# A decoder trunk on one core: who transposes the inverses and the delta rule's output, where the key scales are applied, and the order of the kernel's begin and of the ends of sums

## The chip, the core and the metric

One of the eight cores of a Trainium2 chip runs the whole kernel. The metric is device time in microseconds of one execution, taken as the median over several; a profile shows one execution in detail. The core's engines are TensorE (PE: matrix products and transposes into PSUM, its accumulator memory), VectorE (DVE), ScalarE (ACT), GpSimd (POOL) and SyncE (SP), which here issues nearly all DMAs. Each engine works off its own list of instructions in order and waits for the others by semaphores.

## The reference, cut to what matters

Two layers, 256 tokens of 1024 channels. Each layer is a half-step SwiGLU FFN, a mixer (gated DeltaNet beside a causal convolution module) and another FFN. What the change touches lies in the mixer's delta rule, for chunks of tokens with their decays `G`:

```
kk    = einsum("bhncd,bhnsd->bhncs", k, k)
a_mat = where(strict, kk * decay * beta[..., :, None], 0)
lhs   = eye + a_mat
rhs   = concatenate([v * beta[..., None], k * (beta * exp(G))[..., None]])
u, w  = split(triangular_solve(lhs, rhs, lower=True, unit_diagonal=True))
qk    = einsum("bhncd,bhnsd->bhncs", q, k) * decay
for each chunk:
    v_new = u_c - w_c @ state
    o_c   = q_c @ state + qk_c @ v_new
    state = state * d_c + k_c.T @ v_new
o = rmsnorm(o, norm_w) * silu(z);   y_a = o @ w_o
```

`q` and `k` are L2-normalised per head; there are 8 heads of 128. Each sub-layer ends as `x + r * rmsnorm(f(...), w_post)`, `r` 1/2 for the FFNs and 1 for the mixer.

## The kernel before

**Products.** All large products are float32 made of three passes: weights arrive by DMA as `raw`, ScalarE rounds them to `whi`, VectorE or GpSimd subtracts for `wlo` (`Stream`, lines 246 to 321), activations are split likewise, and `mm3` (543) issues hi x hi, hi x lo and lo x hi. `proj_in` (549) runs over column chunks of an input weight, `proj_out` (610) over contraction steps `kt` of an output weight, 16 x 3 products of 512 columns on the first block of 128 tokens and then as many on the second where there are only 8 steps.

**Order of the work.** TensorE takes its instructions in program order. The program's side work is written as generators ("jobs"), and `Lanes` (177) steps them between products: `lanes.tick()` is called after each group of three 512-column products, `DELAY` gives each job the ticks before its first step and between its steps, `AFTER` and `LATE` say which jobs must be done before and for how many ticks, `BEFORE` and `lanes.finish` force a job to its end at a fixed place, and `FILL` jobs (the 31-tap convolutions on VectorE, the inverse on GpSimd) are stepped whenever a rough model says that the engine has less than `ahead` microseconds of work in front of TensorE. `PLAN` (38) is the order of the mixer's 17 column chunks, with the jobs that each chunk's end starts. From the mixer's second chunk on, up to three chunks before its end, VectorE's and GpSimd's instructions keep program order (`in_order`, 103), and ScalarE's stay behind TensorE's (`Held`, 160); elsewhere a scheduler orders all engines but TensorE by priority and readiness.

**The delta rule.** Tokens are worked on in two blocks of 128 (`tb`), heads in two groups of four (`gp`). `k_tokens` (896) and `q_tokens` (1043) turn `k` and `q` by TensorE, square them and sum for the norms. `similarity` (920) makes `at`, multiplies by `sc` (the key's beta and inverse squared norm) and writes its 32x32 diagonal blocks to DRAM; `inverse` (950) inverts all of them at once on GpSimd and sends them back to `U` by way of DRAM, in eight DMAs per layer (line 974). `merge` (978) joins the blocks to 128x128 inverses by small products: its first four steps transpose `U` by TensorE, one step per head group and block, four heads each, and ScalarE copies three 32x32 diagonal blocks per head out of PSUM into `at`. `scan_first` and `scan_second` (1082, 1100) run the chunk recurrence; `head` (1074) makes four products into one PSUM bank and lets ScalarE copy it out as `vn`, `state` or `o`. The key scale `sc` is in `qk` (multiplied in on VectorE, one head at a time) and, times a decay, in `ktok` (through `kds`).

**The output.** `o_first` and `o_norm` (1288, 1292) norm and gate `o`, block by block; `o_norm` then transposes `o` by TensorE in four groups of four and splits the result to `oT` (`ot` in the profile). This job runs between the products of the convolution's output projection; the projection with `gdn_w_o` follows at once and reads `oT`.

**Begin and ends.** `start` (479) loads `x` in halves, transposes eight 128-column pieces of the first block, multiplies by the norm's weight into `xt`, and takes the first weight piece in two halves of the work but one DMA. `post` (529) ends each sub-layer: per half, a squared sum on ScalarE (`jk`, `ss`) and the weighted copy `fw` on VectorE; then `rms_scale` (414), a small sum on VectorE and a power on GpSimd (`rpost`), and the addition to `x`.

**The activations' turn, as it is.** In `ffn` (649) the gated activations are already transposed without TensorE: VectorE turns 32x32 blocks (`way`), four DMAs write them to DRAM, one reads them back in place.

Of the kernel before, what the change touches and what calls it, by code (L numbers as in the profile page):

```python
# [13 lines left out]
ALU = mybir.AluOpType  # L14
# [8 lines left out]
RING = 8  # L23
RMS_EPS = 1e-6
# [21 lines left out]
    "first": (1, 2), "ffn": (3, 5, 12), "pre0": (13, 7, 8, 4, 3, 3), "pre1": (15, 16, 0, 13, 8),  # L46
    "yt0": (10, 0, 10, 10, 26), "yt1": (10, 2, 0, 3, 3), "f_g0": (5, 0, 2, 1), "f_g1": (5, 1, 1, 1), "c0": (0, 0),
    "f_k1": (0, 1, 3, 1, 1, 3), "f_ka": (2, 0, 3), "decays": (12, 4, 2, 15, 4), "dts": (51, 3, 0, 0, 19, 19),
# [15 lines left out]
    "qs": ("qt0", "qt1"), "s0": ("merge", "vt0", "vt1", "qt0", "qt1"), "s1": ("s0",),  # L64
# [5 lines left out]
FILL = (("c3", "c2", "c1", "c0"), ("inv",))  # L70

LATE = {"inv": 20, "cn": 12, "sim0": 6, "sim1": 6, "merge": 7, "dts": 14}

POOL = {5, 7, 8, 11, 13, 16, *range(18, 21), 23, *range(29, 33), 35, 36, *range(39, 45), *range(47, 50), 51, 53, 55, 58, 60, 61, 63, 65, 67, 68, *range(70, 73), 77, 78, 84, 85}

CFG = dict(stat=500, conv=50, ev=300, tok=4, st=4, post=-800, pre=1000, fin=None, turn=None, tokens=-100, glu=100, dec=200, dts=-100, kt=-400, vt=1000, qt=50, inv=1000, sim=100, merge=-400, scan=50, norm=200, onorm=-100, yt=-400, w=50, tails=4, ahead=1.5, lag=6, free=3, aheadp=3, lag2=3, bias=2, held=1)

KIND = {"f_g0": "glu", "f_g1": "glu", "f_g2": "glu", "f_g3": "glu", "decays": "dec", "dts": "dts", "kt0": "kt", "kt1": "kt",
        "vt0": "vt", "vt1": "vt", "qt0": "qt", "qt1": "qt", "qs": "qt", "inv": "inv", "sim0": "sim", "sim1": "sim",
# [97 lines left out]
class Lanes:  # L177
# [13 lines left out]
    def step(self, job):  # L191
        try:
            with prio(self.tc, KIND.get(job[1])):
                next(job[3])
            job[2] += 1
# [50 lines left out]
class Stream:  # L246
# [16 lines left out]
    def load_one(self, parts=1):  # L263
# [5 lines left out]
        nc.sync.dma_start(raw[:, :n], src)  # L269
# [11 lines left out]
        if self.lanes is not None:  # L281
            c = slice(0, n)
            self.his.append((self.lanes.now + CFG["lag"], i, lambda: high(c)))
            self.lows.append((self.lanes.now + CFG["lag"] + CFG["lag2"], i, lambda eng: low(c, eng)))
            return
        for k in range(parts):
            if k:
                yield
            c = slice(k * n // parts, (k + 1) * n // parts)
            high(c)  # L290
# [1171 lines left out]
```

## Time and profile before

| | |
|---|---|
| median of 3 runs | 1355.97 us (1354.11 to 1357.88) |
| the profiled execution | 1356.38 us |
| its span, first to last instruction | 1354.4 us |
| mean granted TensorE clock | 0.998 |
| DMA: mean rate, HBM read | 202 GB/s, 256.68 MB |

A line of a group reads: source line, engine, operation, tiles written <- tiles read, shapes, count, then busy time in us, mean ns of one, and after the second bar the engine's idle time just before them with what ended it. Source lines 123, 143, 149 and 170 are the helpers through which all instructions of VectorE and GpSimd, all products, all transposes, and all of ScalarE pass, so groups are told apart by their tiles. A row of a timeline is: start, duration, engine, the same description, and in brackets the idle time before it. Products overlap in TensorE's pipeline, so the cost of one is read from start to start and not from its duration.

### The profile page before, as it was taken

To read this page: it belongs to the slowest core of one execution; us is meant where nothing else is said; L and a number is where in the kernel's file an instruction comes from. 1 tells how busy PE (TensorE), PEld (TensorE's weight loads), DVE (VectorE), ACT (ScalarE), POOL (GpSimd) and SP (SyncE) were. 2 spreads that over 40 slices of the span, in tenths; PEclk is the share of its full clock that TensorE was granted. 3 is DMA by queue.
4 is the path that set the end of the run, shared out by engine and by line. 5 is a ranking of instruction groups with operands and counts; after the bars stand their busy time and mean duration, and the time that the engine had idled before them with its cause. 6 is when DMAs were issued, how large, how long until landed. Compare 5 with 4: busy or idle time off the path is not lost.

```text
span 1354.4 us, 20203 instructions
## 1 busy us (share of the span) xinstructions
PE 1331.3 (98%) x7259; PEld 1132.3 (84%) x7259; DVE 926.9 (68%) x1593; ACT 730.8 (54%) x1172; POOL 446.4 (33%) x372
## 2 busy tenths in 40 slices
PE   9999999998999999999999999999989999999998
PEld 7888878997888888888888888799978878888886
DVE  6666456999966676765476654579999566766553
ACT  6554447666555545554455553577555564555541
POOL 0111025798834201111001110278986432011110
PEclk9999999999999999999999999999999999999999
DMA  7877745553634666876478775464545446477760
GB/s 273 284 259 248 232 164 192 185 191 114 196 125 147 212 229 207 281 253 218 148 230 278 263 236 186 143 233 172 172 143 166 151 139 233 157 258 254 257 225 33
DMA packets 114644, 273.76 MB, mean 202 GB/s; under 512 B 24656, under 2 KB 47728, under 8 KB 114544
## 3 DMA queue, kind: packets, MB, share of 16 engines
q1 hardware_dynamic: 114256, 272.40, 60.1%
q8 instruction: 57, 0.93, 0.3%
q14 instruction: 43, 0.35, 0.1%
q10 hardware_dynamic: 288, 0.07, 0.0%
HBM read 256.68 MB, written 15.75 MB: 201 GB/s over the span
## 4 chain that ended last, share of the span: by engine, by line
PE 81%; DVE 9%; POOL 3%; ACT 3%; issue 2%; DMA 1%; DVEq 0%; POOLq 0%; ACTq 0%
PE mm L143 75%; PE gd L143 4%; DVE cacc L123 3%; DVE c L123 3%; PE tr L149 2%; POOL wlo L123 2%; DVE wlo L123 2%; DMA raw<-mw 1%; ACT whi L170 1%; POOL rk L123 1%; DVE at L123 1%; ACT dt L170 1%; PE gd L149 0%; ACT sg L170 0%; ACT cf L170 0%
## 5 line engine op out<-in xcount | busy, mean ns | idle before, releaser
L143 PE MATMUL mm<-whi,xt 128*128 128x512 f32 (+1 forms) x2048 | 648.4, 392 | 4.8 <-ACT qT L170 2.3
L170 ACT CAST whi<-raw 128x1024 fp32r<-128x1024 f32 (+2 forms) x445 | 459.4, 1041 | 321.6 <-PE mm L143 201.4
L123 DVE TENSOR_TENSOR wlo<-raw,whi 128x1024 fp32r<-128x1024 f32 (+1 forms) x341 | 425.0, 1258 | 199.3 <-ACT whi L170 193.5
L143 PEld LDWEIGHTS mm<-whi,xt 128*128 128x128 f32 x2048 | 383.2, 188 | 85.2 <-DVE xt L123 4.9
L143 PE MATMUL mm<-wlo,xt 128*128 128x512 f32 (+1 forms) x1024 | 396.7, 387 | 0.5 <-DVE wlo L123 0.5
L123 POOL TENSOR_TENSOR wlo<-raw,whi 128x1024 fp32r<-128x1024 f32 (+1 forms) x104 | 247.4, 2394 | 142.5 <-ACT whi L170 138.1
L143 PEld LDWEIGHTS mm<-wlo,xt 128*128 128x128 f32 x1024 | 193.1, 189 | 37.2 <-DVE wlo L123 1.0
L143 PE MATMUL mm<-whi,act 128*128 128x512 f32 x704 | 218.3, 390 | 0.0
L123 POOL TENSOR_TENSOR act<-way,act 128x512 fp32r<-128x512 f32 x44 | 78.6, 1785 | 406.1 <-ACT act L170 396.4
L123 DVE SCALAR_TENSOR_TENSOR cacc<-hT,pc,cacc 128x254 f32<-128x254 f32 (+28 forms) x464 | 179.5, 470 | 0.2
L143 PE MATMUL mm<-xt,whi 128*128 128x256 f32 x960 | 175.0, 284 | 0.5 <-ACT qT L170 0.5
L143 PEld LDWEIGHTS mm<-whi,act 128*128 128x128 f32 x704 | 132.2, 188 | 27.5
L143 PEld LDWEIGHTS mm<-xt,whi 128*128 128x128 f32 x960 | 149.5, 192 | 1.2 <-ACT qT L170 0.8
L143 PE MATMUL mm<-wlo,act 128*128 128x512 f32 x352 | 137.0, 389 | 0.0
L143 PE MATMUL mm<-xt,wlo 128*128 128x256 f32 x480 | 135.8, 283 | 0.0
L143 PEld LDWEIGHTS mm<-xt,wlo 128*128 128x128 f32 x480 | 92.0, 192 | 0.0
L170 ACT ACTIVATE ag<-mm,rstd 128x256 f32<-128x256 f32 x88 | 41.8, 475 | 91.3 <-PE mm L143 75.2
L123 DVE SCALAR_TENSOR_TENSOR ag<-mm,rstd,ag 128x256 f32<-128x256 f32 x88 | 42.4, 481 | 54.0 <-ACT ag L170 53.8
L143 PEld LDWEIGHTS mm<-wlo,act 128*128 128x128 f32 x352 | 66.1, 188 | 13.5
L123 POOL TENSOR_TENSOR rpost<-ss,exp 128x1 f32<-128x1 f32 x12 | 6.5, 538 | 194.1 <-DVE ss L123 194.1
L123 DVE SCALAR_TENSOR_TENSOR fw<-mm,wbc 128x512 f32<-128x512 f32 x24 | 16.5, 687 | 46.4 <-ACT jk L170 46.4
L170 ACT ACTIVATE jk<-mm 128x512 f32<-128x512 f32 x24 | 14.4, 598 | 62.3 <-PE mm L143 62.3
(187 smaller groups left out, 1180.7 us busy)
## 6 DMA issues: line engine op xcount, KB each, us to landing
raw<-mw SPq DMA_DIRECT2D x168, 512.0 KB, 3.7
raw<-w1i SPq DMA_DIRECT2D x88, 512.0 KB, 4.7
raw<-w2i SPq DMA_DIRECT2D x88, 512.0 KB, 4.8
raw<-w1o SPq DMA_DIRECT2D x44, 512.0 KB, 4.3
raw<-w2o SPq DMA_DIRECT2D x44, 512.0 KB, 4.2
way<-way SPq DMA_DIRECT2D x176, 64.0 KB, 1.8
way<-way SPq DMA_DIRECT2D x44, 256.0 KB, 4.8
wbc<-feat SPq DMA_DIRECT2D x13, 512.0 KB, 4.5
```

Of the source, the lines that this page charges most:

```text
L123: r = op(out, *a, **k)
L143: r = self.eng.matmul(o, w, x, **k)
L149: r = self.eng.transpose(*a)
L170: r = op(*a, **k)
```

## The change

- **Inverses.** `merge`'s first four TensorE steps become two steps on VectorE: `V.transpose` of the three diagonal blocks of 32x32 for eight heads at a time, from `U` straight into `at`. ScalarE's copies go.
- **Output.** `o_norm` turns each tile of `o` by VectorE in 32x32 blocks (`way`), writes it to DRAM with four DMAs and reads it back with four into `land`; ScalarE and VectorE split `land` into `oT`. TensorE takes no part.
- **Key scales.** `head` gets `tb`: `vn` is made on VectorE as the bank times `sc`. `qk` is then a plain product for four heads at once, `kds` disappears, `ktok` is only multiplied by the decay. `q` times its decay `gx` moves from VectorE to GpSimd. The query's norm becomes a job of its own (`qn0`, `qn1`).
- **Begin.** The first 256 columns of `x` are loaded by themselves, the first two weight pieces in two DMAs each, and two transposes stand ahead of the first product; in the first chunk two pieces run on the first block and then on the second (`lead`).
- **Ends.** In `post` the scale `r` is started before the second `fw`.
- **Order.** `v1` goes before `g2` in `PLAN`; `s1`, `s0`, `on0`, `cn1` and `qs` hang on other chunks; nearly all numbers of `DELAY`, `LATE`, `POOL` and the priorities in `CFG` are new.

The diff's core (`TURN` holds "o" and "u", so the branches for other letters, cut here, are not taken):

```diff
-    ("kb", ["f", "sim0", "kt0", "inv", "c1"]), ("g3", ["f", "c3"]), ("g2", ["f"]), ("v1", ["f", "vt1", "c2"]),
-    ("q0", ["f", "qt0"]), ("q1", ["f", "qt1", "qs", "cn"]), ("v0", ["f", "vt0"]), ("z0", ["s1", "s0"]),
-    ("z1", ["merge"]), ("a0", []), ("b0", []), ("b1", ["on0"]), ("a1", ["cn1", "on"]),
+    ("kb", ["f", "sim0", "kt0", "inv", "c1"]), ("g3", ["f", "c3"]), ("v1", ["f", "vt1", "c2"]), ("g2", ["f"]),
+    ("q0", ["f", "qt0", "qn0"]), ("q1", ["f", "qt1", "qn1", "cn", "s1"]), ("v0", ["f", "vt0"]), ("z0", ["qs"]),
+    ("z1", ["merge", "s0"]), ("a0", ["on0"]), ("b0", []), ("b1", ["cn1"]), ("a1", ["on"]),
...
     "merge": (4, 3, 2, 2, 2, 3, 2, 2)
-    "s0": (12, 6, 0, 0, 17, 17, 25), "s1": (11, 5, 3, 6, 1, 1),
-    "on": (1, 21, 0, 0, 5, 1, 16, 16), "cn1": (0, 0, 4, 0, 6, 3, 0, 1),
+    "s0": (3, 6, 0, 0, 17, 17, 22, 9), "s1": (8, 5, 3, 14, 1, 1, 1),
+    "on": (0, 21, 16, 0, 13, 2, 13, 16), "cn1": (0, 0, 4, 1, 6, 3, 0, 6),
...
     def load_one(self, parts=1):
-        nc.sync.dma_start(raw[:, :n], src)
+        for k in range(parts):
+            c = slice(k * n // parts, (k + 1) * n // parts)
+            nc.sync.dma_start(raw[:, c], src[:, c])
...
-    for hf in range(2):
-        nc.sync.dma_start(x[0][:, hf * 512:hf * 512 + 512], x_in[0:P, hf * 512:hf * 512 + 512])
+    nc.sync.dma_start(x[0][:, 0:2 * P], x_in[0:P, 0:2 * P])
...
         piece = st.load_one(2)
-        half(0, 0)
         next(piece)
+        nc.sync.dma_start(x[0][:, 2 * P:], x_in[0:P, 2 * P:])
+        second = st.load_one(2)
+        next(second)
         nc.sync.dma_start(x[1], x_in[P:2 * P, :])
-        half(0, 1)
+        pair = turn(0, (0, 1))
+        next(piece)
+        next(pair)
...
     def post(tb, acc, wbc, half, fws, jks):
             S.activation(jk[:, cs], acc[hf], AF.Square, scale=D ** -0.5, accum_out=ss[:, hf:hf + 1])
+            if hf:
+                rms_scale(r, ss[:, 0:1], ss[:, 1:2])
             V.scalar_tensor_tensor(fw[:, cs], acc[hf], half, wbc[:, cs], op0=ALU.mult, op1=ALU.mult)
-        r = small(1, "rpost")
-        rms_scale(r, ss[:, 0:1], ss[:, 1:2])
...
+    def turn_out(src, name, t=None):
+        t = tokt("turn") if t is None else t
+        V.transpose(t.rearrange("p (j m t) -> p m j t", j=4, m=4), src.rearrange("p m (j c) -> p m j c", c=32))
+        d = dram.tile([4, 32, 4, P], F32, name=name)
+        for i in range(4):
+            nc.sync.dma_start(d[:, :, i].rearrange("j c w -> c j w"),
+                              t[32 * i:32 * i + 32].rearrange("c (j w) -> c j w", j=4))
+        return d
+    def turn_in_rows(land, d):
+        for m in range(4):
+            nc.sync.dma_start(land[:, m].rearrange("p (i t) -> p i t", i=4),
+                              d.rearrange("j c i (m t) -> m (j c) i t", m=4)[m])
...
         def merge():
-            for gp in (1, 0):
+            for gp in (1, 0) if "u" in TURN else ():
+                for b in (0, 64, 32):
+                    V.transpose(AT[gp][b:b + 32, :, b:b + 32], U[gp][b:b + 32, :, b:b + 32])
+                yield
+            for gp in (1, 0) if "u" not in TURN else ():
...
-                for hl in range(4):
-                    th = tb * 4 + hl
-                    V.scalar_tensor_tensor(qk[:, th, :], ps[:, hl, :], sc[:, gp * 8 + th:gp * 8 + th + 1],
-                                           DT[gp][:, th, :], op0=ALU.mult, op1=ALU.mult)
+                ts = slice(tb * 4, tb * 4 + 4)
+                V.tensor_tensor(qk[:, ts, :], ps, DT[gp][:, ts, :], op=ALU.mult)
-            V.tensor_tensor(qv, qv, GX[gp][:, 4:8, :], op=ALU.mult)
+            W.tensor_tensor(qv, qv, GX[gp][:, 4:8, :], op=ALU.mult)
...
-        def head(gp, fn, tile):
+        def head(gp, fn, tile, tb=None):
-            S.copy(tile, ps)
+            if tb is None:
+                S.copy(tile, ps)
+            else:
+                by = sc[:, gp * 8 + tb * 4:gp * 8 + tb * 4 + 4].rearrange("p (h o) -> p h o", o=1).broadcast_to([P, 4, P])
+                V.tensor_tensor(tile, ps, by, op=ALU.mult)
...
         def o_norm():
             o_scale(1)
+                for tb in range(2):
+                    for gp in range(2):
+                        ds[gp, tb] = turn_out(o[gp][:, tb * 4:tb * 4 + 4, :], f"od{l}{gp}{tb}", way[gp][:, tb])
+                        yield
+                yield CFG["outw"]
+                for gp, tb in ds:
+                    turn_in_rows(land[gp][:, tb], ds[gp, tb])
+                yield CFG["inw"]
+                for gp, tb in ds:
+                    S.activation(hi, src, AF.Copy, scale=nw)
+                    V.scalar_tensor_tensor(lo, src, nw, hi.bitcast(F32), op0=ALU.mult, op1=ALU.subtract)
+                    yield
```

`yield CFG["outw"]` (4) and `yield CFG["inw"]` (8) make a job wait so many ticks.

More of the change, by code (lines that the diff above doesn't have):

```diff
@@ L193, in step @@
             with prio(self.tc, KIND.get(job[1])):
-                next(job[3])
-            job[2] += 1
+                wait = next(job[3])
+            if wait is not None:
+                job[0] = self.now + wait
+                job[2] = job[2] or 0.5
+                return
+            job[2] = int(job[2]) + 1
             d = DELAY[job[1]]
@@ L408, in trunk @@
         pieces += list(m)
-        pieces += [w2i[l, i] for i in range(44)] + [w2o[l, i] for i in range(22)]
+        pieces += [w2i[l, i] for i in range(4 * FC)] + [w2o[l, i] for i in range(2 * FC)]
     def power(o, v, e):
@@ L502, in start @@
         piece = st.load_one(2)
-        half(0, 0)
         next(piece)
+        nc.sync.dma_start(x[0][:, 2 * P:], x_in[0:P, 2 * P:])
+        second = st.load_one(2)
+        next(second)
         nc.sync.dma_start(x[1], x_in[P:2 * P, :])
-        half(0, 1)
+        pair = turn(0, (0, 1))
+        next(piece)
+        next(pair)
+        next(piece)
+        next(pair, None)
+        next(piece)
         next(piece, None)
         def steps():
+            for _ in turn(0, (2, 3)):
+                pass
+            for _ in second:
+                pass
+            yield
             half(1, 0)
+            st.load()
+            yield
+            half(0, 1)
             st.load()
@@ L532, in post @@
         ss = small(2, "ss2")
+        r = small(1, "rpost")
         for hf in range(2):
@@ L599, in proj_in @@
             ps = [None if c < first else ps_mm(), ps_mm()]
-            for i in range(8 // chunks[c][1]):
+            b = 2 if lead and c == 0 else 1
+            for i in range(0, 8 // chunks[c][1], b):
                 for tb in range(c < first, 2):
-                    piece(c, tb, i, ps[tb], st.peek(0))
-                st.done()
+                    for j in range(b):
+                        piece(c, tb, i + j, ps[tb], st.peek(j))
+                for j in range(b):
+                    st.done()
             with prio(tc, "ev"):
@@ L683, in fin @@
             lanes.add("ffn", steps())
-        proj_in(xt, [(512, 2)] * 11, ev, fin, first)
+        proj_in(xt, [(512, 2)] * FC, ev, fin, first, lead=not first)
         wbc = load_feat(l, wpost, 17)
@@ L694, in done @@
             after(tb)
-        proj_out(lhs, 22, done, tails)
+        proj_out(lhs, 2 * FC, done, tails)
     def mixer(xt, l, after_mix):
@@ L1027, in v_tokens @@
         def v_tokens(gp):
-            vT, t = vr[gp], slot(14 + gp, [P, 8, P], name="vr")
-            vr[gp] = t
-            for tb in range(2):
+            vT, t = vr[gp], slot(14 + gp, [P, 2, 512], name="vr")
+            vr[gp] = t.rearrange("p b (i m t) -> p b m i t", i=4, m=4)
+            ds = []
+            for tb in range(2) if "v" not in TURN else ():
                 if tb:
@@ L1043, in q_tokens @@
         def q_tokens(gp):
-            sq = slot(18 + gp, [P, 8, P], name="sq")
-            ss = small(8, "ssk")
-            yield from by_tokens(qT[gp], 0, sq, ss)
-            yield
-            yield from by_tokens(qT[gp], 1, sq, ss)
-            V.tensor_scalar(vq[:, gp * 8:gp * 8 + 8], ss, float(P), P * 1e-6, op0=ALU.mult, op1=ALU.add)
+            ss = QN[gp] = small(8, "ssq")
+            if "q" in TURN:
+                ds = [turn_out(qT[gp][:, :, tb * P:(tb + 1) * P], f"qd{l}{gp}{tb}") for tb in range(2)]
+                QN[gp] = (ss, ds)
+            else:
+                sq = slot(18 + gp, [P, 2, 512], name="sq")
+                for tb in range(2):
+                    if tb:
+                        yield
+                    tr = ps_tr()
+                    for hl in range(4):
+                        T.transpose(tr[:, hl, :], qT[gp][:, hl, tb * P:(tb + 1) * P], ident)
+                    yield from squares(sq[:, tb], tr, tb, ss)
             qk = slot(18 + gp, [P, 8, P], name="qk")
@@ L1174, in take @@
             staged = stage.pop(c) if c in by_ch else [stage.pop((c, tb)) for tb in range(2)]
+            if c not in by_ch and "g" in TURN and name != "ka":
+                way = slot(10 + c, [P, 2, 512], name="way")
+                ds = [turn_out(staged[tb].rearrange("p (m c) -> p m c", m=4), f"sd{l}{c}{tb}",
+                               way[:, tb]) for tb in range(2)]
+                yield CFG["outw"]
+                land = slot(14 + c, [P, 4, SEQ], name="land")
+                for tb in range(2):
+                    turn_in_rows(land[:, :, tb * P:(tb + 1) * P], ds[tb])
+                yield CFG["inw"]
+                staged = {j: land[:, j] for j in range(4)}
             if kind == "g":
```

177 lines of the change are left out of this document (124 added, 53 removed), and 17 rows, old and new, of the table DELAY.

## The prediction

> **What bounds the kernel now.** I read the page first: its busy times and the chain that ended last.
>
> ```profile
> span 1354.4 us, 20203 instructions
> PE 1331.3 (98%) x7259; PEld 1132.3 (84%) x7259; DVE 926.9 (68%) x1593; ACT 730.8 (54%) x1172; POOL 446.4 (33%) x372
> PE 81%; DVE 9%; POOL 3%; ACT 3%; issue 2%; DMA 1%; DVEq 0%; POOLq 0%; ACTq 0%
> ```
>
> TensorE is busy for 98% of the span, so what comes off its instruction list comes off the time, unless something else is late at the same place. The profiled execution took 1356.38 us, 0.41 above the median of 1355.97, and 1.98 us of it lie outside the span. I make the sum against 1356.38 and subtract 0.41 at the end.
>
> Next, the groups of PE by shape (count, busy, mean ns), because the change deletes two of them:
>
> ```profile
> L149 PE MATMUL tr<-cst,o 128*128 128x128 f32 x32 | 4.8, 272 | 0.0
> L149 PE MATMUL gd<-cst,u 128*128 128x128 f32 x32 | 4.8, 272 | 0.0
> ```
>
> The 272 ns are latencies that overlap with the neighbours. The price is in the starts, so I took PE's timeline around one group of each kind (start, duration):
>
> ```profile
> 442.35 0.60 PE L149 MATMUL tr<-cst,o 128*128 128x128 f32 x4
> 442.70 0.48 PE L143 MATMUL mm<-whi,xt 128*128 128x512 f32 x1
> ...
> 443.48 0.60 PE L149 MATMUL tr<-cst,o 128*128 128x128 f32 x4
> ...
> 446.21 0.62 PE L143 MATMUL mm<-whi,xt 128*128 128x512 f32 x2
> ...
> 446.89 0.62 PE L143 MATMUL mm<-whi,xt 128*128 128x512 f32 x2
> ```
>
> ```profile
> 355.42 0.60 PE L149 MATMUL gd<-cst,u 128*128 128x128 f32 x4
> ...
> 357.95 0.60 PE L149 MATMUL gd<-cst,u 128*128 128x128 f32 x4
> ...
> 359.77 0.60 PE L149 MATMUL gd<-cst,u 128*128 128x128 f32 x4
> ```
>
> From 446.21 to 446.89 three products pass in 0.68 us. From 442.35 to 443.48 four transposes and three products pass in 1.13: the four cost 0.45. From 357.95 to 359.77 it is 1.82 for four transposes and six products (two such triples, 1.36): 0.46. Nothing waits in either stretch; here PE really runs without a hole.
>
> The third view is PE's list of waits (total, times, longest), which says where TensorE is not the bound:
>
> ```profile
> PE tr L149 <- ACT cf L170: 3.4, 2, 1.7
> PE tr L149 <- ACT vT L170: 2.9, 2, 1.5
> PE mm L143 <- ACT qT L170: 2.8, 4, 1.1
> PE tr L149 <- ACT sq L170: 1.7, 2, 0.8
> PE mm L143 <- DVE xt L123: 1.6, 4, 0.5
> PE tr L149 <- ACT stg L170: 1.0, 2, 0.6
> ```
>
> They sum to 13.4 us over both layers. All stand in the mixer, where VectorE takes its instructions in a written order and runs behind.
>
> **Transposes off TensorE.** Per layer, `merge` loses four groups on `u` (two head groups by two blocks) and `o_norm` four on `o`; two layers make 8 x 0.46 + 8 x 0.45 = 7.3 us. Each sits between products, so the whole comes off the path if the data arrive as early as the shorter list wants them.
>
> **The inverse's turn on VectorE.** Six VectorE transposes of 256 columns per layer replace 16 on PE and twelve copies on ScalarE. Their nearest row is the gated activations' turn; behind it the rows of what VectorE does at that place, and of PE's products it waits for:
>
> ```profile
> L123 DVE STREAM_TRANSPOSE way<-ag 128x256 f32<-128x256 f32 x88 | 37.5, 437 | 2.9
> ```
>
> ```profile
> 350.86 1.95 PE L143 MATMUL gd<-qT,kT 128*128 128x128 f32 x16
> ```
>
> ```profile
> 356.81 2.15 DVE L123 SCALAR_TENSOR_TENSOR qk<-gd,sc,dt 128x128 f32<-128x128 f32 x8
> 358.88 0.68 DVE L123 TENSOR_TENSOR qT<-qT,gx 128x512 f32<-128x512 f32 x1
> ```
>
> The products end at 352.81 and VectorE comes to them at 356.81: its queue is 4.0 us behind. `merge` begins at 355.42, and its first product now comes after 4 + 3 + 2 ticks instead of 4 + 3 + 2 + 2 + 2, five ticks after the first turn: 5 x 0.68 = 3.4 us of cover. With the queue 4.0 behind, the three turns of the first head group end at 355.42 + 4.0 + 3 x 0.44 = 360.7, 1.9 us after the 358.8 at which PE asks. The change also shortens this queue: `qk` becomes two plain products of 512 columns instead of eight of 128 (2 x 0.69 for 2.15, by the row of `fw` below), and `qT` times `gx` (0.68) goes to GpSimd, together 1.45. The wait is then 1.9 - 1.45, about 0.5 us per layer. The bounds are 0 (queue caught up) and 1.9. What can also be late is the inverse itself, read back by these DMAs:
>
> ```profile
> L974 SPq DMA_DIRECT2D u<-dU x8: 337/432/462, 345.0 to 353.7; - x8
> DMA to landing us min/median/max: 3.0/4.6/5.3
> ```
>
> The last is issued at 353.7 and lands by the median at 358.3. VectorE now wants it in the second step of `merge`, 3 ticks after 355.42, at 357.5, and PE at 360.2; turning takes 1.3, so the two arrive together and I add nothing. I take +1.0 us for both layers.
>
> **The output's way through DRAM.** Per tile of 512 columns: one VectorE turn (twice the 0.44), four DMAs out, four in, and the cast and rest that stood there before. When the second block's output is ready and when PE wants the first is in these rows:
>
> ```profile
> 435.58 0.87 DVE L123 SCALAR_TENSOR_TENSOR o<-o,ro,z 128x128 f32<-128x128 f32 x3
> ```
>
> ```profile
> 451.00 0.39 PE L143 MATMUL mm<-whi,ot 128*128 128x512 f32 x1
> ```
>
> ```profile
> way<-way SPq DMA_DIRECT2D x176, 64.0 KB, 1.8
> ```
>
> Ready at 436.45, wanted at 451.0. The shorter list moves the demand to 451.0 - 8 groups (3.6) = 447.4 and the readiness, behind the four groups on `u`, to 434.6: 12.8 us of cover for the first block and, as `proj_out` runs 16 x 3 products (10.9) on it first, 23.7 for the second. Trip of the second block's two tiles: turns 1.8, eight issues out at 0.43 (3.4), landing 1.8, eight issues in (3.4), landing 4.6 (the nearest row with 128-byte pieces is `u<-dU`, half as large), cast and rest 1.4 (two operations of 512 columns like `fw`): 16.4 of 23.7. The first block is ready a scan step earlier, since `on0` finishes it, and has only to be sent before. So I cost it at nothing; hidden by the convolution's projection. Without that cover it costs up to 16.4 per layer.
>
> The Trainium skill speaks against this step: "VectorE: DVE Perf Modes", section The three transpose paths, gives VectorE only 32x32 blocks and calls a plain strided DMA used as a transpose 19 times slower than its own path, and section Rules for kernel authors sends a 128x128 transpose to TensorE. Here the four groups on TensorE cost 1.8 us per layer against a trip of 16.4, so in latency the trace agrees; in TensorE time it is the other way round.
>
> **Key scales.** `vn` leaves ScalarE for a VectorE product, 4 per layer; the `kds` step on GpSimd goes and GpSimd gets `qT` times `gx`. None of it touches PE's list; nothing in the sum, and a rival below.
>
> **The end.** The last rows of the timeline:
>
> ```profile
> 1347.71 0.60 ACT L170 ACTIVATE jk<-mm 128x512 f32<-128x512 f32 x1 [2.03 <-PE mm L143]
> 1348.20 0.19 ACT L170 ACTIVATION_READ_ACCUMULATOR jk<-mm 128x1 f32 x1
> 1348.43 0.69 DVE L123 SCALAR_TENSOR_TENSOR fw<-mm,wbc 128x512 f32<-128x512 f32 x1 [2.03 <-ACT jk L170]
> 1349.04 0.20 DVE L123 TENSOR_SCALAR ss<-ss 128x1 f32<-128x1 f32 x1
> 1349.38 0.54 POOL L123 TENSOR_TENSOR rpost<-ss,exp 128x1 f32<-128x1 f32 x1 [10.34 <-DVE ss L123]
> ```
>
> `ss` now goes ahead of `fw`: it starts at 1348.43 instead of 1349.04, and `fw` runs beside GpSimd's 0.54: -0.6 us. The same in the other posts may take some of the 1.6 on `xt`; I count none.
>
> **The beginning.** Two transposes, two casts and half a weight piece stand before the first product instead of eight, four and a half piece cut from a whole DMA:
>
> ```profile
> 4.29 1.91 PE L149 MATMUL tr<-cst,x 128*128 128x128 f32 x8
> 5.39 1.14 ACT L170 ACTIVATE xt<-tr,first_w 128x128 fp32r<-128x128 f32 x4 [2.73 <-PE tr L149]
> 6.41 0.63 ACT L170 CAST whi<-raw 128x512 fp32r<-128x512 f32 x1
> 7.09 0.80 PE L143 MATMUL mm<-whi,xt 128*128 128x512 f32 x1 [0.89 <-ACT whi L170]
> ```
>
> Half of the 1.14 and, with the weight cast ahead of it, up to the 0.63 go: the first product comes up to 1.2 us sooner. But the second block of `x` is now loaded behind the second weight piece, and its transposes stand after the second contraction step in PE's order. That is two more issues of 0.43 ahead of it. I take -0.5, between -1.2 and +0.9.
>
> **The clock.** Right behind the second layer's waits on `vT` and `sq` the windows show (PE busy, PEld, DVE, ACT, POOL, granted clock):
>
> ```profile
> 1000.60:1004.00 3.40, 1.75 (x12) 1.32 (x13) 3.40 (x8) 2.70 (x9) 3.01 (x6) 1.00 0.00 0
> 1004.00:1007.40 3.40, 3.40 (x17) 3.21 (x16) 3.37 (x9) 1.36 (x4) 3.17 (x5) 0.50 0.00 0
> ```
>
> After 3.4 us of which TensorE was busy for 1.75, its clock was halved for 3.4: 1.7 us lost. The change may have it none or two times: nothing in the sum, 1.7 either way in the bounds.
>
> **Sum.** -7.3 + 1.0 + 0 - 0.6 - 0.5 = -7.4: 1349.0 for the profiled execution, 1348.6 for the median. Its bounds: -7.3 - 0.6 - 1.2 - 1.7 = -10.8 and -7.3 + 3.8 - 0.6 + 0.9 + 1.7 = -1.5, so 1345 to 1354.
>
> **The rivals.** (a) *The mixer's waits shrink too.* `v1` moves two places from `q0`, VectorE has less in its order, `cn1` and `qn` have other places. If half of the 13.4 goes: 1348.6 - 6.7 = 1342. Against it: `v0` and `z0` stay neighbours, and `BEFORE` still forces `qt0` at `z0`.
>
> (b) *VectorE's queue takes the gain.* `merge` and `vn` now wait for a queue that was 4.0 behind. The turns' 1.9 instead of 0.5, and `vn`: its second use allows 3 ticks, 2.0 us, where 4.0 behind and two products of 0.69 need 5.4, at most 3.4 late. With 1.4 + 2.3 more per layer the gain is 0: 1356. For it: the row at 356.81. Against it: `qk` and `gx` lighten this queue.
>
> (c) *The trip comes late: slower.* SyncE issues all DMAs in one queue, weights too. In the stretch of the mixer's second half its own list of waits has
>
> ```profile
> SPq L368 <- PE mm L143: 8.8, 1, 8.8
> ```
>
> a load of a norm's weights that stood 8.8 us for a slot PE had still to release, with all behind it. If the way out or in stands behind such a load, or the first block's way in behind the second's way out, PE waits at the output projection. It decides from (7.4 + 4.1) / 2 = 5.8 us per layer; at 8.8 the time is 1348.6 + 17.6 = 1366.
>
> (d) *Strided DMAs do not overlap.* Sixteen in per layer at 4.6 each, one after another, make 74 against 23.7 of cover: +50 per layer, 1449. Against it: eight `u<-dU` were issued within 8.7 us of each other and none took over 5.3. [...]
>
> **How the numbers follow.** A measurement tells about 0.3% (4.1 us) from no change. Forecast 0.58, of which 0.03 lies above 1351.9, within 0.3%; (a) 0.15; (b) 0.14; (c) 0.11; (d) 0.02. Faster is the rest of the forecast and (a), 0.70; same is (b) and that 0.03, 0.17; slower (c) and (d), 0.13. From 1341 to 1358 lie the forecast, the milder half of (a), (b) and the mild end of (c); the other half of (a), most of (c) and (d), about 0.2, are left out.
>
> **What would show it.** Right: PE's groups `tr<-cst,o` and `gd<-cst,u` gone, PE's list of waits without a new row on `ot` and with at most 2 us on `at`, the first `mm<-whi,ot` following its predecessor at 0.23 us, the first product before 6.5 us, `ss` ahead of `fw`. Wrong: a wait of PE on `ot` (c), on `at` or `vn` (b), or the six rows of PE's waits halved (a).

## The result and the profile after

The changed kernel takes 1364.05 us (median of 4, 1362.25 to 1365.26) where the kernel before takes 1356.24 on the same chip: ratio 1.0057, 95% interval [1.0039, 1.0076]. It is slower, by 7.8 us, where 7.4 less was forecast. The profiled execution took 1365.26. From its page, the span, the busy times and the chain that ended last:

```profile
span 1363.5 us, 20204 instructions
PE 1332.5 (98%) x7195; PEld 1132.4 (83%) x7195; DVE 926.8 (68%) x1596; ACT 725.1 (53%) x1137; POOL 433.6 (32%) x370
PE 82%; DVE 6%; DMA 4%; POOL 3%; ACT 2%; issue 2%; SPq 1%; POOLq 0%; DVEq 0%; ACTq 0%
```

TensorE has 64 instructions fewer and is busy for longer. The list of PE's waits (total, times, longest) says where it stands now:

```profile
PE tr L154 <- ACT cf L175: 6.6, 2, 3.3
PE gd L148 <- DVE at L128: 4.6, 4, 2.0
PE tr L154 <- ACT vT L175: 3.7, 2, 1.9
PE tr L154 <- DMA x<-x: 2.2, 2, 1.4
```

Two rows are new (`at`, `x`) and one has doubled (`cf`, 3.4 before). None is on `ot`. The second half of the loss is the clock. Windows of the changed kernel (us, then busy time of PE, PEld, DVE, ACT, POOL, then the granted clock), around the first layer's merge and its convolution norm:

```profile
357.93:361.35 3.42, 1.33 (x19) 0.79 (x18) 2.17 (x7) 1.04 (x1) 3.42 (x2) 1.00 0.85 217
361.35:364.76 3.41, 1.75 (x18) 1.59 (x19) 2.20 (x3) 2.49 (x5) 3.41 (x3) 0.50 0.64 168
364.76:368.18 3.42, 3.24 (x30) 2.26 (x29) 3.33 (x7) 0.27 (x1) 3.31 (x2) 0.50 0.80 286
368.18:371.59 3.41, 3.41 (x19) 2.31 (x16) 3.41 (x8) 1.77 (x3) 1.51 (x5) 0.50 0.48 169
371.59:375.00 3.41, 3.41 (x58) 2.99 (x57) 3.41 (x10) 1.13 (x3) 2.31 (x1) 1.00 0.11 36
```

```profile
429.61:433.03 3.42, 0.09 (x1) 0.00 (x0) 3.29 (x6) 3.42 (x9) 0.00 (x0) 1.00 0.64 199
433.03:436.44 3.41, 3.40 (x10) 2.79 (x11) 2.74 (x7) 2.80 (x10) 0.55 (x1) 0.50 0.47 154
```

A window in which TensorE is busy for 1.33 or 0.09 of 3.41 us is followed by one at half clock, and merge stays there for three: in the first of them PE stands again (1.75 busy), but the second is busy for 3.24 and the third is still at half clock (the last section comes back to this). To see what each costs, I divided the time of TensorE's list, from one start to the next: the median interval of that shape in the kernel before (content), idle time over 0.1 us that the profile gives a releaser (waits), what is left inside stretches at half clock (half), and what is left elsewhere (rest); the time before 14.1 us counts as half clock. The last column is when the last product starts. The rows of all runs stand here together; "time" is the ratio to the kernel before on the same chip, the other columns are of the one profiled execution. The zeros of e8 and e11 (products added to keep TensorE busy, see there) are priced at 427 ns, the interval of that shape at the kernel's start, where the clock is half; in e8's merge eight of them took 1.83 us, so the content of these two runs is some 2 to 4 us too high, and the rest as much too low.

| kernel | time, 95% interval | content | waits | half | rest | last product |
|---|---|---|---|---|---|---|
| before | 1 | 1312.9 | 14.9 | 6.1 | 12.1 | 1347.3 |
| after | 1.0057 [1.0039, 1.0076] | 1305.9 | 23.0 | 14.5 | 12.0 | 1356.7 |
| e1 U only | 1.0085 [1.0066, 1.0104] | 1309.4 | 24.0 | 11.9 | 12.7 | 1359.3 |
| e2 output only | 1.0154 [1.0137, 1.0171] | 1309.4 | 28.6 | 12.8 | 11.7 | 1363.8 |
| e3 no turn | 1.0153 [1.0138, 1.0168] | 1312.9 | 29.0 | 10.2 | 12.7 | 1366.1 |
| e4 old numbers | 1.0024 [1.0012, 1.0036] | 1305.9 | 21.1 | 7.1 | 13.9 | 1349.4 |
| e5 before, U, end | 1.0033 [1.0021, 1.0044] | 1309.4 | 20.1 | 8.6 | 10.9 | 1350.3 |
| e6 e5 and output | 1.0043 [1.0029, 1.0057] | 1305.9 | 22.5 | 12.0 | 12.4 | 1354.2 |
| e7 inverse earlier | 1.0405 [1.0389, 1.0420] | 1305.9 | 65.9 | 21.0 | 10.9 | 1404.9 |
| e8 zeros in merge | 1.0046 [1.0033, 1.0059] | 1311.9 | 16.9 | 10.3 | 9.0 | 1349.4 |
| e9 cast after norm | 1.0032 [1.0015, 1.0050] | 1305.9 | 19.4 | 8.5 | 12.4 | 1347.5 |
| e10 U turned early | 0.9964 [0.9952, 0.9977] | 1309.4 | 15.2 | 5.4 | 11.5 | 1342.8 |
| e11 e9 and zeros | 1.0031 [1.0018, 1.0044] | 1317.9 | 17.5 | 4.7 | 10.1 | 1351.6 |
| e12 e10 and zeros | 0.9961 [0.9949, 0.9973] | 1312.5 | 12.7 | 2.8 | 11.3 | 1340.5 |
| e13 e10 and output | 0.9981 [0.9972, 0.9989] | 1305.9 | 19.0 | 4.4 | 12.6 | 1343.1 |
| e14 begin only | 1.0073 [1.0059, 1.0086] | 1312.9 | 18.4 | 10.4 | 13.5 | 1356.6 |
| e15 e7, own queue | 1.0321 [1.0302, 1.0339] | 1305.9 | 48.0 | 20.7 | 13.0 | 1388.8 |

By this count, which prices the 64 transposes at 110 ns, the median from start to start, the forecast's -7.3 on TensorE is there as -7.0. Against it stand +8.1 of waits and +8.4 of half clock. By place, waits and half clock together: first layer's merge +8.1, second's +0.7; the two convolution norms +1.6 and +1.6 of waits and +1.6 and +2.9 of half clock. The single executions of one kernel differ by the half clock too: the eleven of e5 lie between 1356.5 at a mean granted clock of 0.994 and 1365.4 at 0.988.

### The profile page after: what moved, and what is told of

Its sections match the earlier page's. It is cut to its first block, busy times and chain, and to the rows that moved or that the text cites. A ratio compares the mean times of both kernels' runs of the same rounds, so it can differ in the third digit from the quotient of the medians.

```text
span 1363.5 us, 20204 instructions
## 1 busy us (share of the span) xinstructions
PE 1332.5 (98%) x7195; PEld 1132.4 (83%) x7195; DVE 926.8 (68%) x1596; ACT 725.1 (53%) x1137; POOL 433.6 (32%) x370
## 4 chain that ended last, share of the span: by engine, by line
PE 82%; DVE 6%; DMA 4%; POOL 3%; ACT 2%; issue 2%; SPq 1%; POOLq 0%; DVEq 0%; ACTq 0%
PE mm L148 76%; PE gd L148 4%; DVE cacc L128 3%; POOL iu L128 2%; PE tr L154 2%; DMA raw<-mw 2%; DVE wlo L128 1%; ACT whi L175 1%; POOL wlo L128 1%; DVE c L128 1%; DMA u<-dU 1%; DMA land<-od 1%; DMA x<-x 0%; DVE at L128 0%; DMA ia<-dA 0%
## 5 line engine op out<-in xcount | busy, mean ns | idle before, releaser
L128 DVE TENSOR_TENSOR wlo<-raw,whi 128x1024 fp32r<-128x1024 f32 (+2 forms) x344 | 418.5, 1223 | 266.4 <-ACT whi L175 261.2
L128 POOL TENSOR_TENSOR wlo<-raw,whi 128x1024 fp32r<-128x1024 f32 (+1 forms) x102 | 239.8, 2359 | 183.2 <-ACT whi L175 181.8
L128 POOL TENSOR_TENSOR act<-way,act 128x512 fp32r<-128x512 f32 x44 | 75.7, 1720 | 412.7 <-ACT act L175 391.7
L175 ACT ACTIVATE jk<-mm 128x512 f32<-128x512 f32 x24 | 14.3, 597 | 61.0 <-PE mm L148 61.0
L128 DVE SCALAR_TENSOR_TENSOR c<-mm,pc,c 128x255 f32<-128x255 f32 (+2 forms) x108 | 43.4, 473 | 2.0 <-ACT c L175 2.0
```

The lines of the kernel that those rows point to most:

```text
L128: r = op(out, *a, **k)
L175: r = op(*a, **k)
```

## The experiments

### Turns or numbers: e1 to e4

The change sets new numbers for the order (plan, delays, lags, fillers, priorities, splits) beside the new code. Theory A: the turns make the waits. Theory B: the numbers do. Three runs take turns out of the changed kernel, the fourth takes the numbers out:

```
-TURN = set("ou")
+TURN = set("u")      # e1;  set("o") is e2, set("") is e3
```

> The changed kernel, with the output turned on TensorE again (U still on VectorE); all else, the order's numbers included, as changed. Theory A (the turns themselves make the new waits): the wait on at (4.6 us and about 5.7 us of half clock behind it) stays, the longer wait of the convolution's norm (3.2 us and about 4.5 us of half clock) goes with the output's casts on ScalarE and VectorE, and the eight groups on o come back (3.6): 1364 - 7.7 + 3.6 = 1360. Theory B (the new numbers of the order, which start the inverse later and force the norm, make them, whatever turns): 1364 + 3.6 = 1368, with both waits in place.

> The changed kernel, with U turned on TensorE again (the output still by way of DRAM). Theory A: no wait on at, no half clock behind it (4.6 + 5.7 go), eight groups on u come back (3.7): 1364 - 10.3 + 3.7 = 1357. Theory B: TensorE's own transposes now wait for the same late read-back of u, the half clock stays: 1364 + 3.7 = 1368.

> The changed kernel with neither turn: all sixteen groups on TensorE, all else as changed. Theory A: both clusters of waits go, the groups come back: 1364 - 18 + 7.3 = 1353. Theory B: the waits stay and the groups come back: 1371.

In words, as the lists are long, e4 is:

```
-PLAN, DELAY, FILL, LATE, POOL, CFG of the changed kernel
+those of the kernel before, "qn0"/"qn1" behind "qt0"/"qt1"; "on", "first", "ffn" as changed
```

> The changed kernel with both turns, but with the plan, delays, lags, fillers, priorities and weight splits of the kernel before (only the steps that did not exist there, and those of the output's turn and of the start, keep the new numbers). Theory A: the waits come with the turns: about 1364. Theory B: the inverse is as early as before and the norm's wait 1.7 each: the forecast's -7.4 with the begin's +1.2 instead of -0.5, 1350 to 1351.

Measured: 1367.1, 1375.0, 1375.4 and 1358.4 us, with the kernel before at 1354.9. The first is B's to 1 us, the second and third lie 7 and 4 beyond B: without the turns, the new numbers are far slower. PE's waits of e2 and e3:

```profile
PE gd L154 <- DMA u<-dU: 11.3, 2, 6.6
```

```profile
PE gd L154 <- DMA u<-dU: 10.8, 2, 6.2
```

With U on TensorE, its own transposes stand 11 us for the read-back of the inverse. In the kernel before there is no such wait: there GpSimd works on `iu` from 302.0 to 341.5 us, in the changed kernel from 316.7 to 352.9. With the old numbers (e4) it is 304.3 to 343.3, and PE has no wait on `at`. So the late inverse comes with the numbers, and VectorE's turn is the quicker one behind it: it is worth 0.0097 (e2 to after, 13 us), more than its eight groups.

One thing is A's: in e1 and e3, without the output's trip, PE's wait on `cf` is 1.7 per layer again, half of the changed kernel's 3.3. So e1 meets B's time to 1 us in part by luck: B had both waits in place. What stands there instead is a wait on `ot`, 4.6 us in e1 and 4.0 in e3, which neither the kernel before nor the changed one has. PE's waits of e1:

```profile
PE mm L148 <- ACT ot L175: 3.2, 2, 2.0
PE mm L148 <- DVE ot L128: 1.4, 2, 0.8
```

And e4 is 7 to 8 us above what B gave. Its waits are 6.2 longer than before's, on `vT` first of all, and behind `vT` both layers have 6.83 us at half clock, where before has 3.41 in one (e14 comes back to this):

```profile
PE tr L153 <- ACT vT L174: 5.1, 4, 1.8
PE tr L153 <- ACT cf L174: 3.4, 2, 1.7
```

### One turn at a time in the kernel before: e5 and e6

```
-                    for hl in range(4):
-                        T.transpose(pt[:, hl, :], U[gp][:, tb * 4 + hl, :], ident)
-                    for b in (0, 64, 32):
-                        S.copy(at[b:b + 32, ts, b:b + 32], pt[b:b + 32, :, b:b + 32])
+                for b in (0, 64, 32):
+                    V.transpose(AT[gp][b:b + 32, :, b:b + 32], U[gp][b:b + 32, :, b:b + 32])
```

with the new `post`; e6 has the change's `o_norm`, `turn_out`, `turn_in_rows` and `head_part` as well.

> The kernel before, with two things of the change alone: U turned on VectorE (the eight groups on u and the twelve copies per layer on ScalarE go), and ss ahead of the last fw at the ends of the sums. The order's numbers are those of before. Theory B (the late read-back, made by the new numbers, is what cost the turn of U): no wait on at, -3.7 - 0.6 = -4.3 against the kernel before, 1350 to 1351. Theory C (VectorE's written order holds the turn up wherever it stands): a wait on at of 1.9 per layer and a half clock of 3.4 us behind it (1.7): +3.8 + 3.4 - 4.3, 1357 to 1358.

> As the run before, with the output's way through DRAM as well (its steps' delays as in the change). Theory B (the longer wait of the convolution's norm comes from the trip and the new numbers together; with the old ones the norm waited 1.7 as ever): another -3.6, so 1346 to 1347, with the rest of the change (key scales, other layouts, the start) then costing the 11 to 12 us up to the 1358 of the changed code under the old numbers. Theory R (the trip's casts on ScalarE and VectorE cost what the transposes cost): 1350 to 1351, no better than without it.

Measured: 1358.3 and 1361.3. In e5 theory B fails and theory C has it, with a longer wait than its 1.9: with the old numbers and the inverse as early as ever, the turn waits in VectorE's own order.

```profile
PE gd L143 <- DVE at L123: 5.1, 2, 2.5
```

VectorE's timeline of e5 shows what stands ahead of it. The last `u` landed at 354.1:

```profile
354.09 2.15 DVE L123 SCALAR_TENSOR_TENSOR qk<-gd,sc,dt 128x128 f32<-128x128 f32 x8
356.16 0.68 DVE L123 TENSOR_TENSOR qT<-qT,gx 128x512 f32<-128x512 f32 x1
356.76 1.54 DVE L123 SCALAR_TENSOR_TENSOR cacc<-hT,pc,cacc 128x228 f32<-128x228 f32 x4
358.21 1.36 DVE L123 STREAM_TRANSPOSE at<-u 32x256 f32<-32x256 f32 x3
359.60 1.24 DVE L123 TENSOR_TENSOR wlo<-raw,whi 128x1024 fp32r<-128x1024 f32 x1
360.77 1.36 DVE L123 STREAM_TRANSPOSE at<-u 32x256 f32<-32x256 f32 x3
```

The wait is the same 2.5 us in both layers. In the first it costs just that; in the second a stretch of 13.65 us at half clock follows it and costs 6.3 more. In e6 it is the other way round, the first layer has the 13.65. Which of the two it hits is a matter of where the wait falls. e6 lies above both of its forecasts; with the trip it is no better than e5, as theory R says in kind, but the two intervals overlap.

### The inverse earlier: e7 and e15

```
-LATE = {"inv": 22, "cn": 13, "sim0": 12, "sim1": 7, "merge": 1, "dts": 16}
+LATE = {"inv": 20, "cn": 13, "sim0": 6, "sim1": 6, "merge": 1, "dts": 14}
```

and the old delays of `kt0`, `kt1`, `sim0`, `sim1`, `dts`, `inv`; e15 also issues the DMAs of `dU` by `nc.gpsimd` instead of `nc.sync`.

> The changed kernel with the old numbers for the steps ahead of the inverse alone (delays of the keys' and similarities' steps, the masks and the inverse, and their lags: 6, 6, 20 and 14 instead of 12, 7, 22 and 16), so that the inverse ends some 6 us earlier against TensorE's order. Theory B: the wait on at (4.6) and the half clock behind it in the first layer (4.2) go, 1364 - 8.8 = 1355. Theory C: the wait on at stays as it is, 1364.

> The run with the earlier inverse (which took 1411 because SyncE stood up to 28 us for iu with all weight loads behind it), with the ten DMAs of the inverse per layer issued by GpSimd instead of SyncE, so that nothing of the weights stands behind them. If the late read-back is what TensorE waits for at the merge: the wait on at (4.6) and the half clock behind it in the first layer (4.2) go, 1364 - 8.8 = 1355, and the 45 us on vT are gone. If VectorE's order holds the turn anyway: 1364. If the weights are not what stood: vT waits on, 1400 or more.

Measured: 1411.0 (1.0405 [1.0389, 1.0420]) and 1397.9 (1.0321 [1.0302, 1.0339]). Both miss, and say another thing. In e7 SyncE's list has the write of `iu` ahead of weight loads; ScalarE stands 25.2 us for weights with the activation of `vT` behind its casts, and PE for `vT`. SyncE's row, and PE's:

```profile
SPq L1040 <- POOL iu L128: 54.4, 2, 28.4
```

```profile
PE tr L154 <- ACT vT L175: 45.3, 2, 22.9
```

In e15 that is gone, but GpSimd now holds its weight splits behind those DMAs: SyncE waits up to 30.8 us for a split on GpSimd to release its buffer, and PE 10.6 on `z` per layer. Whichever queue carries the wait for the inverse, what is behind it is late. Which of the new numbers puts the inverse late was not found. One that bears on the same wait was not tried alone: `LATE` of `merge`, the ticks that `merge` has to stay behind the inverse, goes from 7 to 1 in the change, and e7 and e15 keep the 1. Six ticks are 4.1 us at 0.68 per group of three products; whether this number holds `merge` anywhere in these plans is not shown.

### The clock: e8 and e11

```
                at, ps[gp] = AT[gp], ps_gd([P, 16, 32])
+                for _ in range(8 if l == 0 else 0):
+                    nc.tensor.matmul(ps[gp].rearrange("p a b -> p (a b)"), idle[:, 0:P], idle[:, P:640], start=True, stop=True)
```

> The changed kernel with sixteen products of zeros on TensorE in the first layer's merge, eight ahead of each head group's products on at, where TensorE waits 1.7 and 2.0 us for VectorE; they write PSUM that the next products overwrite. If the halved clock is the price of the wait: the stretch of 10.2 us at half clock behind the merge goes, -4.2, 1360. If the clock falls whatever TensorE does there: the stretch stays, 1364.

Measured: 1361.8, by time alone not to be told from the changed kernel (the intervals overlap; the profiled execution, 1358.0, is the fastest of the four). The windows tell it: at the same place the clock stays full.

```profile
356.85:360.26 3.41, 3.36 (x16) 2.13 (x16) 1.34 (x4) 1.21 (x2) 3.41 (x2) 1.00 0.84 208
360.26:363.68 3.42, 3.42 (x44) 2.31 (x42) 3.15 (x9) 2.60 (x5) 3.42 (x3) 1.00 0.81 273
363.68:367.09 3.41, 3.36 (x43) 2.30 (x43) 3.41 (x7) 0.80 (x3) 3.41 (x2) 1.00 0.71 219
```

From the first product on `at` (360.65) to the first on `vr` (384.88) it is 24.2 us, zeros included; in the changed kernel (360.32, 388.83) it is 28.5. The zeros add nothing to the result, and take off the 4.2 us that the half clock cost there. e11 is e9 with zeros in both layers' merges and in the waits on `vT`:

```
                for hl in range(4):
+                    for _ in range(14 if gp == 0 and tb == 0 and hl == 2 else 0):
+                        nc.tensor.matmul(tr[:, 2:4, :].rearrange("p a b -> p (a b)"), idle[:, 0:P], idle[:, P:P + 256], start=True, stop=True)
                    T.transpose(tr[:, hl, :], vT[:, hl, tb * P:(tb + 1) * P], ident)
```

> The run with the casts behind the norm, and products of zeros wherever TensorE stands in the second half of the mixer: eight (first layer) and four (second) ahead of each head group's products on at, and fourteen of 256 columns between the second and the third transpose of vT. If each halved stretch is the price of a wait that leaves TensorE idle: 1364 - 7.7 - 4.2 (merge) - 2.2 (behind vT in the second layer) = 1350. If the zeros only move the halved stretch elsewhere: 1356.

Measured: 1358.8. Half clock falls from 14.5 to 4.7, nearly all of it at the two ends, but the time doesn't follow: PE comes sooner to the merge and waits there for the same late `u`.

```profile
PE gd L148 <- DVE at L128: 4.9, 2, 3.0
```

So in the changed kernel the inverse sets that time; the half clock was in part time that PE would have waited. The zeros also take time themselves where TensorE has no wait to fill.

### The output's casts: e9

```
                 yield CFG["inw"]
+                while "cn" not in lanes.done:
+                    yield 1
...
-                    S.activation(hi, src, AF.Copy, scale=nw)
+                    r = S.activation(hi, src, AF.Copy, scale=nw)
+                    behind(tc, getattr(r, "ins", r), normed[3])
```

`normed[3]` is the last cast of `ct` in the norm's first block; the loop lets the output's job wait until the norm's job `cn` is done. e11 has both as well.

> The changed kernel with one more order of the program: ScalarE's two casts of the output's first block stand behind the convolution norm's activations instead of ahead of them. TensorE's order and SyncE's are unchanged. Theory F (the output's way through DRAM is late, and its wait, 2.15 us of ScalarE standing for land, holds the gates, a weight cast and cf behind it): the two waits of 3.3 on cf go back to 1.7, and the half clock behind them (1.6 and 2.9) goes with them: 1364 - 3.2 - 4.5 = 1356, without a new wait on ot. Rival (the norm is late by the new numbers, and the casts only stand beside it): both waits stay, 1364.

ScalarE's timeline of the changed kernel shows what is meant:

```profile
428.95 0.72 ACT L175 ACTIVATE ot<-land,pc 128x512 fp32r<-128x512 f32 x1 [2.15 <-DMA land<-od]
429.58 1.06 ACT L175 ACTIVATE gate<-mm 128x512 f32<-128x512 f32 x2
430.54 1.04 ACT L175 CAST whi<-raw 128x1024 fp32r<-128x1024 f32 x1
431.47 1.51 ACT L175 ACTIVATE cf<-tr,pc 128x128 f32<-128x128 f32 x4
```

ScalarE stands 2.15 us for the trip, and gates, a weight cast and `cf` come behind. Measured: 1357.8, ratio 1.0032 [1.0015, 1.0050], which overlaps the changed kernel's interval; the places tell more than the time. PE's waits of e9:

```profile
PE tr L154 <- ACT cf L175: 3.4, 2, 1.7
```

No half clock follows the norm in either layer, and there is no row on `ot`. Theory F has it, the rival falls.

### Versions that gain: e10, e12, e13

```
-    "merge": (4, 3, 2, 2, 2, 3, 2, 2)
+    "merge": (0, 3, 6, 2, 2, 3, 2, 2)
```

in e5; e12 adds the zeros on `vT` shown above, at the same place in this kernel. VectorE's list has all six turns of U directly behind `qT` times `gx`.

> The kernel before with U turned on VectorE and the new end of the sums, as in the run that had only these, but merge starts four ticks sooner and its first products one tick later against TensorE's other products: VectorE then turns U ahead of four steps of the convolution (1.5) and of a weight split (1.2). Theory C (VectorE's place in its written order is what TensorE waited 2.5 us for): a wait on at of 0.3 to 0.4 per layer, no half clock behind it, 1355 - 3.7 - 0.6 + 0.7 = 1351. If instead whatever TensorE gains comes back as another wait further on: 1354 to 1358.

> The kernel before with U turned early on VectorE, the new end of the sums, and fourteen products of zeros in the wait on vT (1.45 us per layer). By the clock's rule as the runs so far show it (a stretch of 3.41 us in which TensorE is busy for less than about half is followed by one at half clock): no halved stretch between the start and the end, 1.7 less than the same kernel without the zeros, 1349 to 1350. If the clock doesn't hang on this: no better than without them.

Measured: 1350.4 and 1349.9, ratios 0.9964 and 0.9961: both beat both kernels, and the forecast of e10 is met to 1 us. PE's wait on `at` in e10:

```profile
PE gd L143 <- DVE at L123: 0.4, 1, 0.4
```

The zeros of e12 take the half clock from 5.4 to 2.8 us, none of it now between the start and the end; in the median that is 0.5, less than the two measurements can tell apart.

> The run with U turned early under the old numbers, with the output's way through DRAM as well, its first casts on ScalarE held behind the convolution norm's activations. If the trip is worth its eight groups once nothing stands behind its wait: 1350.4 - 3.6 = 1346.8. If the way of the output costs ScalarE, VectorE and SyncE what it saves TensorE, as in the run with the trip under the old numbers (1361 against 1358 without it): 1350 or more.

e13 is e10 with the output's trip and e9's order of the casts (`behind`, without the loop). Measured: 1352.1, ratio 0.9981, no better than without. TensorE's content falls by 3.5, and PE waits as much longer for VectorE:

```profile
PE mm L145 <- DVE wlo L125: 3.2, 5, 0.8
...
PE mm L145 <- DVE ct L125: 1.4, 2, 0.7
```

VectorE now has the turn and the rest of `ot` between the splits of weights and the halves of `ct`: the trip costs VectorE what it saves TensorE.

### The begin: e14

In words:

```
-    start(), the loads of x, load_one, proj_in; "first": (1, 2), "ffn": (3, 5, 12)
+    those of the change; "first": (1, 1, 4, 4, 3, 2, 2), "ffn": (15, 1, 12, 12, 12)
```

> The kernel before with the new beginning alone (first two blocks of x and two half weight pieces first, the rest of x behind them). The forecast's term: -0.5, 1354.4. By the profile of the changed kernel, whose mixer began 1.15 us later: 1356. By the six other profiles with the new beginning (191.4 to 193.9 us at the mixer's first product, against 190.6 to 192.5 with the old one): no difference beyond 0.1%.

Measured: 1365.6, 10.6 us more; none of the three expected that. At the start itself it is 1.6 (the mixer's first product at 193.85 instead of 192.24). The rest arises in the mixers, whose code is the same. Another order of steps in the first FFN shifts the planner's clocks, and GpSimd's work falls otherwise: counted from the mixer's first product, it begins `iu` after 113.4 us instead of 109.8, and a weight split that stands within it comes at 130.4 instead of 125.6. In both kernels this split meets one of VectorE's; what changes is which begins first. In the kernel before it is VectorE's, and GpSimd's takes longer:

```profile
317.82 1.22 DVE L123 TENSOR_TENSOR wlo<-raw,whi 128x1024 fp32r<-128x1024 f32 x1
```

```profile
317.87 3.42 POOL L123 TENSOR_TENSOR wlo<-raw,whi 128x1024 fp32r<-128x1024 f32 x1
```

In e14 it is GpSimd's, and VectorE's takes 2.99 instead of 1.22 us, ahead of `z0`:

```profile
324.76 2.99 DVE L123 TENSOR_TENSOR wlo<-raw,whi 128x1024 fp32r<-128x1024 f32 x1
```

```profile
324.28 2.40 POOL L123 TENSOR_TENSOR wlo<-raw,whi 128x1024 fp32r<-128x1024 f32 x1
```

PE then waits 6.3 us on `vT` over both layers (2.9 before) and is at half clock for 6.83 us behind each. With the 1.6 at the start, these 3.4 of waits and 4.4 of half clock account for the 9.3 by which the last product comes later. That this one collision makes them was not tried. But e4, the one other run with the new beginning under the old numbers, has the same collision in both layers (GpSimd's splits begin at 321.01 and 991.04), and the same half clock behind `vT`. VectorE's rows:

```profile
322.03 2.46 DVE L127 TENSOR_TENSOR wlo<-raw,whi 128x1024 fp32r<-128x1024 f32 x1
...
991.52 3.00 DVE L127 TENSOR_TENSOR wlo<-raw,whi 128x1024 fp32r<-128x1024 f32 x1
```

So most of what e4 lies above theory B (2.2 of waits on `vT` and 4.3 of half clock there, of 7 to 8 us) stands where the beginning costs it in e14. The changed kernel, with new numbers, has no such collision ahead of `z0`; e14 doesn't say what the beginning costs there.

## Why the prediction was wrong

**Transposes off TensorE, -7.3: right in size.** -7.0 by the table's count. That "the whole comes off the path if the data arrive as early as the shorter list wants them" was right too, and they did not. Where they do (e10), U's eight groups and the new end, -4.3 by the forecast's terms, are -4.5 (-3.1 to -6.5).

**The inverse's turn, +1.0: the step that failed.** The prediction took the landing of `u`, 358.3, from an issue and a median delay in the trace of before (in that trace it is 356.8) and put "the two arrive together and I add nothing". The change's own numbers start the inverse 14.7 us later and end it 11.4 later; the last `u` lands at 363.3. VectorE's timeline of the changed kernel:

```profile
358.18 1.65 DVE L128 SCALAR_TENSOR_TENSOR cacc<-hT,pc,cacc 128x254 f32<-128x254 f32 x4
359.75 0.42 DVE L128 STREAM_TRANSPOSE at<-u 32x256 f32<-32x256 f32 x1
362.51 0.90 DVE L128 STREAM_TRANSPOSE at<-u 32x256 f32<-32x256 f32 x2 [2.34 <-DMA u<-dU]
```

PE's wait is 4.6 over both layers, and 4.2 of half clock behind the first. Of the two long waits the second (2.03) ends with the turn that VectorE begins as the read-back lands; the first (1.72) is in part the queue's, as VectorE comes to its turn behind four steps of the convolution, 0.7 us after the first `u` landed at 359.04. The queue that the prediction did price, "0.5 us per layer" with an upper bound of 1.9, is 2.5 where it stands alone (e5). The sum had no term for the numbers, though `DELAY`, `LATE` and the splits are lines of the diff like the others. That they put the inverse late is shown (e2, e3, e4). But the old ones in their place (e4) take off only 0.0033, 4 to 5 us of the 15 between forecast and result; the waits then stand elsewhere, at `vT`.

**The output's trip, 0: right for TensorE, wrong for ScalarE.** PE's list has no row on `ot`: `proj_out`'s cover holds. What was not asked is who stands behind the trip's own casts: the gates and `cf`, +3.2 of waits and 4.5 of half clock. The prediction named the work that hides the trip from PE, and not the queue in which its wait stands.

**The end, -0.6:** from the last product to the end of the span 7.1 us became 6.8. **The begin, -0.5:** the first product came 1.7 us sooner (5.39), more than the 1.2 forecast, but TensorE then waited 0.77 and 1.45 for the rest of `x` behind the weight pieces, and the mixer began 1.15 later (part of this can be the single execution: in the other profiles that place lies at 191.5 to 194.0 with the new beginning, at 190.7 to 192.5 with the old). **Key scales, 0:** not tried alone; PE's list has no row on `vn`.

**The clock, 1.7 either way:** the mis-sized bound. It was taken from one stretch; the changed kernel has four in its mixers, 3.4 to 10.2 us long, where the prediction allowed one more or one less.

**The rivals.** (b) named the place, the wait on `at`, with the lesser cause for this kernel: VectorE's queue has a part of one wait, the landing has the rest; in e5 it is just the queue. The wait on `vn` that (b) added, 2.3 per layer, did not come. (c) put its lateness on `ot` and at the output projection; the trip was late, and the wait stood at the norm. (a) fell as a sum: the six rows make 14.3 instead of 13.4. `qT`'s 2.8 is gone, but `cf` doubled and `vT` grew from 2.9 to 3.7. (d) fell: eight read-backs were issued from 417.97 to 425.30 and each landed within 4.6 us of its issue. The trip took TensorE no time in itself, though it gained none either (e13). The Trainium skill's "VectorE: DVE Perf Modes", section The three transpose paths, has its factor of 19 against the DMA's own transposing path, and for large strides in the destination; these read-backs write pieces of 128 bytes, and no run here has that path, so the factor is not tested.

## What to carry to other kernels

Price a retuned order like an added instruction: look where its new numbers put the latest producer (here GpSimd's inverse), before any landing is taken from the old trace. When work leaves the bound engine for one that runs a written order, the gain is worth what that order has free at that place, and moving the turn ahead of 2.8 us of other VectorE work turned +3.3 us (e5) into -4.5 (e10). A wait of TensorE in a stretch that is otherwise full costs itself, and by chance its own length or more again in clock.

## What the runs showed of the hardware

**The clock's windows.** All halved stretches in the mixers are 3.41 us long or a multiple (6.83, 10.24, 13.65; 27.3 in e7). I laid that grid through the edges of the clock's record in 17 profiles and took TensorE's busy time in each window that ran at full clock. All 28 windows with under 1.5 of 3.41 us were followed by a halved one, of 111 between 2.0 and 2.9 just one was, and of 54 between 1.5 and 2.0 eighteen. So a wait of 2 us or less can halve the clock if it falls whole into one window, and not if two windows share it; two waits of 1.72 on `cf` in the kernel before stood right at this edge. The first:

```profile
423.70:427.10 3.40, 1.68 (x12) 1.32 (x11) 3.27 (x8) 3.25 (x9) 0.55 (x1) 1.00 0.57 167
427.10:430.50 3.40, 3.40 (x18) 2.68 (x17) 2.00 (x4) 3.40 (x19) 0.00 (x0) 1.00 0.42 148
```

The Trainium skill ("TensorE: Matmul & The Clock Gate", Part 1) has such a free-running window of about 3.4 us, and the runs agree; its advice, in the section on why this matters for kernels, to avoid idle gaps over some 3 us is too mild by these windows.

**Why a merge stays at half clock.** Of the halved windows in the mixers, 58 have TensorE busy for 2.9 us or more. In 37 of them no product of `merge`'s 32x32 or 64x64 blocks runs, and 36 of these were followed by full clock. In the other 21 the small products take, from start to start, 0.3 to 0.9 us in eight, which were all followed by full clock, and 0.95 to 1.9 us in thirteen, which were all followed by another halved window. So one wait costs more ahead of small products: the 2.5 us in e5's second layer were followed by four halved windows, busy to the full.

**VectorE beside GpSimd.** A VectorE split that starts during one on GpSimd ends 1.1 us after it, as in e14's two rows (324.28 + 2.40 = 326.68; 327.75); a GpSimd split that starts during one on VectorE ends 2.2 us after it, as in the rows of before (317.82 + 1.22 = 319.04; 321.29). Over the 17 profiles it is 1.08 to 1.15 in 120 such pairs and 2.23 to 2.31 in 40. The Trainium skill ("SBUF — State Buffer", section SBUF: two separate sides) states an exclusive port that the loser waits for; the rows agree.
